# The opening of a two-layer decoder trunk: root on columns of tokens, no POOL, a fourth gate tile, three rounds per tile, unread products on TensorE

## The chip, the cores and the metric

One core of a Trainium2 chip. The metric is the device time of one execution of the whole kernel in microseconds, the median of repeated runs.

## The reference

A trunk of two layers on 512 tokens of 1024 channels, all in float32. Layer 0 mixes tokens by retention (4 heads, rotary positions on q and k), layer 1 by an mLSTM; each is followed by a convolutional FFN. Ahead of each mixer and FFN stands a norm that is modulated by the condition `c`. What matters here is the first of them and the projections that follow it:

```
c_act = silu(c)
mod = c_act @ ada_w[0] + ada_b[0]           # 6 x 1024: shift, scale, gate, twice
h = x * rsqrt(mean(x*x, channels) + 1e-6) * norm_g * (1 + scale) + shift
proj = h @ w_in                             # q, k, v, g
q, k = rope(q, positions), rope(k, positions) / 16
y = group_norm(retention(q, k, v));  x = x + gate * ((silu(g) * y) @ w_out)
```

## The kernel before, in words

**Layout.** Tokens lie along the free axis: `x` is eight tiles of 128 channels by 512 tokens, and a sum over channels is a product with a matrix of ones. Every large product is made of three products of 32-bit operands that are split into a high and a low part (`mm3`, L281 to L283: high x high, low x high, high x low). The high part of a weight is a rounding copy on ACT (L164, in the opening L1165), the low part a subtraction on DVE (L169, in the opening L1169). Activations are split in `parts`: `h.hi` on ACT (L341), `h.lo` on DVE (L343), from `xr`, the scaled tile (L332).

**Modulation.** Each 128 values of `mod` need one pass of DVE over a 128x1025 tile of `ada` (`gemv`, L140: multiply by `silu(c)`, spread on all partitions in `c_ext`, and sum). In the opening three of these are made on POOL (multiply, L144) and ACT (sum, L145) instead. `gain` (L158) is `norm_g * (1 + scale)`, one column.

**The opening** (`ret_start`). Eight tiles of `x` are squared (ACT; the last two on DVE, L1140), pairs are added on DVE (L1145), and four products with ones (L1146) spread the mean of squares to all partitions, 128x512. ACT takes the root (L1190), DVE the reciprocal in two halves (L1196, L1199). Then for each of the eight channel tiles k: two `gemv`s (scale and shift of the tile), `gain`, `scaled`, `parts`, the split of the weight tile `w_s0[k]` (128x896: 512 columns of head 0's values and 3 x 128 of its gate), and 21 products of 512 columns that add into seven PSUM banks: 4 token tiles of values (L1175 to L1177) and 3 gate tiles (L281 to L283). POOL makes the first steps of the tables for the rotary positions meanwhile (`rope_tables`, L1020 to L1034; from L1039 on DVE). DVE, ACT and POOL keep the written order here; PE does not.

**After the opening** the work is a list of items. The first is the projection of the fourth gate tile (`w_in0[7]`), then q and k of head 0 and the first half of head 1's (`proj_item`, 24 products of 512 columns each), and then head 0's scores. A planner orders each engine's instructions by priority (the order of writing) and by its own estimate of when their operands are ready; on an engine they then run in that order. Weights are loaded up to four items ahead into one of six buffers, which the opening's `ada` and weight tiles share. The scores of head 0 need the rotated q and k, and these need the finished tables.

Of the kernel before, what the change touches and what calls it, by code (L numbers as in the profile page):

```python
# [70 lines left out]
def trunk(ctx: ExitStack, tc: tile.TileContext, xT, cb, pos, vec, decay, zmask, ada, w_s0, w_in0, w_v0,  # L71
# [70 lines left out]

    def gemv_pool(layer, f, raw):
        G.tensor_tensor(raw, raw, c_ext[:], op=ALU.mult)  # L144
        A.activation(raw, raw, AF.Copy, accum_out=mods[layer][:, f : f + 1])  # L145
# [871 lines left out]
    def rope_tables():  # L1017

        a, k, k1, r = (slot(n) for n in ("ra", "rk", "rk1", "rr"))
        G.tensor_copy(a[:], posi[:])  # L1020
        G.tensor_scalar(r[:], a[:], col("inv", 0), None, op0=ALU.mult)
        yield
        G.tensor_scalar(k[:], r[:], INV_2PI, None, op0=ALU.mult)
        yield
        ks = []
        for bits in (20, 10):
            big = ROUND * 2.0**bits
            G.tensor_scalar(k1[:], k[:], big, big, op0=ALU.add, op1=ALU.subtract)
            G.tensor_tensor(k[:], k[:], k1[:], op=ALU.subtract)
            yield  # L1030
            ks.append(k1)
            k1 = slot("rk2")
        n = slot("rn")
        G.tensor_scalar(n[:], k[:], ROUND, ROUND, op0=ALU.add, op1=ALU.subtract)  # L1034
        ks.append(n)
        yield
# [10 lines left out]
        turns()  # L1047
        for i, j in ((3, 0), (3, 1), (0, 2), (2, 1), (1, 2), (0, 3), (2, 2), (3, 2)):
            less(i, j)
# [76 lines left out]
    def ret_start():  # L1126

        pss, ps, rs = [], bank("pms"), slot("rs")
        A.activation(rs[:, :1], eps_t[:], AF.Silu)
        one = ones["1"][:1, :].bitcast(F32)  # L1130
        pcs = [bank("pc") for _ in range(2)]
        for i in range(2):
            PE.matmul(pcs[i][:], one, c_row[:1, i * T : i * T + T], start=True, stop=True)
        def mean_squares():
            sq = [slot("sq") for _ in range(KT)]
            for m in range(KT):
                if m < 6:
                    A.activation(sq[m][:], x[m][:], AF.Square)
                else:
                    V.tensor_tensor(sq[m][:], x[m][:], x[m][:], op=ALU.mult)  # L1140
                if m == 5:
                    for i in range(2):
                        A.activation(c_ext[:, i * T : i * T + T], pcs[i][:], AF.Silu)
                if m % 2:
# [37 lines left out]
        with tc.manual_schedule(engines={mybir.EngineType.DVE, mybir.EngineType.Activation, mybir.EngineType.Pool}):  # L1182
# [18 lines left out]
            for k in range(KT):  # L1201
                if k + 1 < KT:
                    for f in (KT + k + 1, k + 1):
                        load_ada(f)
                    if k + 2 < KT:
                        load_raw(k + 2)
# [310 lines left out]
```

## Time and profile before

| | |
|---|---|
| median of 3 runs | 1560.03 us (1559.39 to 1560.14) |
| the profiled execution | 1554.46 us |
| its span, first to last instruction | 1552.7 us |
| mean granted clock of TensorE | 0.992 |
| PE, DVE, ACT, POOL busy | 97%, 77%, 55%, 15% of the span |
| first product of the opening | 16.66 us after the span's start |
| granted clock, 15 to 20 and 20 to 25 us | 0.68 and 0.63 |

PE is TensorE's matmuls, PEld its weight loads, DVE is VectorE, ACT ScalarE, POOL GpSimd, SP the engine whose queue issues the loads. A row of a timeline gives start, length, engine, line, operation, tiles and shapes, and in brackets how long the engine had been idle and what released it. A row of the windows gives a stretch, its length, the busy time and count of instructions of PE, PEld, DVE, ACT and POOL, the granted clock, the DMA share and GB/s. Lengths of matmuls include the time in the pipeline; their pace is read from start to start.

### The profile page before, as it was taken

The page shows a single profiled execution, that of the slowest core. Times are in us where ns is not written, and L with a number is a line of the kernel's source. Part 1 is how long each engine was busy: PE and PEld are TensorE (multiplying, and loading weights), DVE is VectorE, ACT ScalarE, POOL GpSimd, SP SyncE. Part 2 cuts the span into 40 slices and gives each one's busy share as a digit, 9 for nine tenths or more (in the row PEclk, how much of TensorE's full clock was granted, in tenths as well). Part 3 has the DMA queues.
Part 4 walks back from the last instruction along what each step waited for, and adds up shares of the span by engine and source line. Part 5 has one row for each costly group of instructions (what it writes and reads, how often), then busy time and mean ns, then how long its engine had stood idle before and what let it go on. Part 6 is the DMA issues. An engine that isn't in the chain of part 4 may idle for free. (4 is left out here: it accounts for less than half of the span.)

```text
span 1552.7 us, 23173 instructions
## 1 busy us (share of the span) xinstructions
PE 1513.2 (97%) x8996; PEld 1337.2 (86%) x8996; DVE 1200.5 (77%) x1814; ACT 861.2 (55%) x1282; POOL 229.3 (15%) x242
## 2 busy tenths in 40 slices
PE   7999999999999999999999999999999999999997
PEld 4788888888988999998988878888889889999997
DVE  8985768786997878887777777777588977787775
ACT  4534524443456767676655554554545666767763
POOL 3421001110130111111110011001022201111102
PEclk9999999999999999999999999999999999999999
DMA  8753464655315888887444433443312258777751
GB/s 312 228 186 109 143 188 159 204 177 167 110 42 136 210 208 205 230 195 202 160 128 149 149 109 105 152 144 112 126 54 72 67 135 198 195 191 188 187 140 55
DMA packets 72224, 241.79 MB, mean 156 GB/s; under 512 B 9761, under 2 KB 12065, under 8 KB 72114
## 3 DMA queue, kind: packets, MB, share of 16 engines
q1 hardware_dynamic: 59730, 195.22, 38.4%
q0 software_dynamic: 12384, 45.09, 15.3%
q8 instruction: 70, 1.15, 0.3%
q14 instruction: 40, 0.33, 0.1%
HBM read 193.06 MB, written 2.12 MB: 126 GB/s over the span
## 5 line engine op out<-in xcount | busy, mean ns | idle before, releaser
L164 ACT CAST whi<-raw 128x1024 fp32r<-128x1024 f32 (+1 forms) x190 | 194.3, 1029 | 144.4 <-PE pp L282 58.3
L169 DVE TENSOR_TENSOR wlo<-raw,whi 128x1024 fp32r<-128x1024 f32 (+1 forms) x158 | 191.5, 1219 | 46.7 <-ACT whi L164 46.1
L281 PE MATMUL pp<-hh,whi 128*128 128x512 f32 x560 | 218.4, 390 | 2.3 <-DVE vl L278 2.0
L282 PE MATMUL pp<-hl,whi 128*128 128x512 f32 x560 | 218.1, 390 | 0.0
L283 PE MATMUL pp<-hh,wlo 128*128 128x512 f32 x560 | 218.0, 389 | 0.0
L595 DVE SCALAR_TENSOR_TENSOR x<-po,mod,x 128x512 f32<-128x512 f32 (+1 forms) x184 | 114.2, 629 | 71.6 <-PE po L283 68.0
L282 PE MATMUL po<-ggl,whi 128*128 128x512 f32 (+1 forms) x448 | 154.0, 345 | 0.0
L283 PE MATMUL po<-ggh,wlo 128*128 128x512 f32 (+1 forms) x448 | 153.5, 344 | 0.0
L281 PE MATMUL po<-ggh,whi 128*128 128x512 f32 (+1 forms) x448 | 153.0, 345 | 0.0
L422 PE MATMUL p<-hh,whi 128*128 128x256 f32 x544 | 150.6, 277 | 0.0
L423 PE MATMUL p<-hl,whi 128*128 128x256 f32 x544 | 150.4, 276 | 0.0
L424 PE MATMUL p<-hh,wlo 128*128 128x256 f32 x544 | 150.4, 276 | 0.0
L140 DVE SCALAR_TENSOR_TENSOR ada<-ada,c_ext 128x1025 f32<-128x1025 f32 x93 | 115.7, 1245 | 32.3 <-DMA ada<-ada 32.2
L281 PEld LDWEIGHTS pp<-hh,whi 128*128 128x128 f32 x560 | 105.2, 188 | 24.6 <-DVE vl L278 2.5
L283 PEld LDWEIGHTS pp<-hh,wlo 128*128 128x128 f32 x560 | 105.2, 188 | 21.8
L282 PEld LDWEIGHTS pp<-hl,whi 128*128 128x128 f32 x560 | 105.2, 188 | 21.4
L281 PE MATMUL po<-yh,whi 128*128 128x256 f32 (+1 forms) x352 | 115.8, 329 | 0.0
L282 PE MATMUL po<-yl,whi 128*128 128x256 f32 (+1 forms) x352 | 115.6, 328 | 0.0
L283 PE MATMUL po<-yh,wlo 128*128 128x256 f32 (+1 forms) x352 | 115.6, 328 | 0.0
L927 ACT ACTIVATE cv<-p,vecs 128x512 f32<-128x512 f32 x68 | 53.1, 780 | 96.2 <-PE p L424 57.3
L932 DVE SCALAR_TENSOR_TENSOR cv<-p,vecs,cv 128x511 f32<-128x511 f32 (+1 forms) x136 | 101.0, 745 | 2.2
L422 PEld LDWEIGHTS p<-hh,whi 128*128 128x128 f32 x544 | 102.2, 188 | 0.1
(287 smaller groups left out, 3986.9 us busy)
## 6 DMA issues: line engine op xcount, KB each, us to landing
ada<-ada SPq DMA_DIRECT2D x96, 512.5 KB, 4.0
raw<-w_in SPq DMA_DIRECT2D x62, 512.0 KB, 3.8
wb<-w_up SPq DMA_DIRECT2D x34, 512.0 KB, 4.4
wa<-w_up SPq DMA_DIRECT2D x34, 512.0 KB, 5.3
wlo<-wa POOLq DMA_DIRECT2D x34, 512.0 KB, 4.6
wlo<-ws POOLq DMA_DIRECT2D x34, 512.0 KB, 4.9
raw<-w_o SPq DMA_DIRECT2D x32, 512.0 KB, 3.5
raw<-w_dn SPq DMA_DIRECT2D x32, 512.0 KB, 4.4
```

The costliest lines, as they stand in the source:

```text
L140: return V.scalar_tensor_tensor(raw, raw, 1.0, c_ext[:], op0=ALU.mult, op1=ALU.mult, accum_out=mods[layer][:, f : f + 1])
L164: A.copy(hi, w[:, r])
L169: V.tensor_tensor(lo, w[:, r], hi.bitcast(F32), op=ALU.subtract)
L281: PE.matmul(o, ah, bh, start=start, stop=False)
L282: PE.matmul(o, ah, bl, start=False, stop=False)
L283: PE.matmul(o, al, bh, start=False, stop=stop)
L422: PE.matmul(o, hi[:, ch], b[0], start=st, stop=False, skip_group_check=True)
L423: PE.matmul(o, hi[:, ch], b[1], start=False, stop=False, skip_group_check=True)
L424: PE.matmul(o, lo[:, cl], b[0], start=False, stop=sp, skip_group_check=True)
L595: V.scalar_tensor_tensor(x[m][:, r], ps[:, r], gate_col, x[m][:, r], op0=ALU.mult, op1=ALU.add)
L927: A.activation(acc[:], ps[:], AF.Identity, bias=col("fcb", self.layer * 2 * FT + f), scale=self.conv_col(f, 2))
L932: V.scalar_tensor_tensor(acc[:, s:], ps[:, : T - s], self.conv_col(f, j), acc[:, s:], op0=ALU.mult, op1=ALU.add)
```

## The change

- The mean of squares is made the other way round: the squared tile is the loaded weight and one column of ones the moving operand, so that four products per pair give the mean as a 128x4 block, a column for each 128 tokens (`means`). Tiles 0 to 5 are added in pairs, 6 and 7 stand alone. Root and reciprocal are taken on 128x4, four copies of an identity are scaled by the columns, and two products with ones spread the result to 128x512 in PSUM, from which ACT copies it to SBUF.
- POOL has no arithmetic left in the opening: all sixteen `gemv`s are on DVE; the rope tables are wholly on DVE (but for the cosine's last step), and are made after the opening, as item 0 and after the first q product.
- The weight tile holds the fourth gate tile too (128x1024, eight banks); the item `w_in0[7]` goes.
- The 24 products of a tile run in three rounds: high x high for all eight banks, then high x low, then low x high.
- PE keeps the written order in the opening, and 13 products that nobody reads (`busy`) stand between the steps: 5 of 128 columns at the start, 3 after the sums, 5 before the first tile.
- The loads are reordered: an identity and the first columns of `vecs` ahead, the rest of `vecs` after the loads of tiles 0 to 2 but the third weight tile, `posi` last.

```diff
-    def gemv_pool(layer, f, raw):
-        G.tensor_tensor(raw, raw, c_ext[:], op=ALU.mult)
-        A.activation(raw, raw, AF.Copy, accum_out=mods[layer][:, f : f + 1])
...
     def rope_tables():
-        G.tensor_copy(a[:], posi[:])
-        G.tensor_scalar(r[:], a[:], col("inv", 0), None, op0=ALU.mult)
-        yield
-        G.tensor_scalar(k[:], r[:], INV_2PI, None, op0=ALU.mult)
-        yield
+        V.tensor_copy(a[:], posi[:])
+        V.tensor_scalar(r[:], a[:], col("inv", 0), None, op0=ALU.mult)
+        V.tensor_scalar(k[:], r[:], INV_2PI, None, op0=ALU.mult)
         ks = []
         for bits in (20, 10):
             big = ROUND * 2.0**bits
-            G.tensor_scalar(k1[:], k[:], big, big, op0=ALU.add, op1=ALU.subtract)
-            G.tensor_tensor(k[:], k[:], k1[:], op=ALU.subtract)
-            yield
+            V.tensor_scalar(k1[:], k[:], big, None, op0=ALU.add)
+            V.tensor_scalar(k1[:], k1[:], big, None, op0=ALU.subtract)
+            V.tensor_tensor(k[:], k[:], k1[:], op=ALU.subtract)
...
-        G.tensor_scalar(n[:], k[:], ROUND, ROUND, op0=ALU.add, op1=ALU.subtract)
+        V.tensor_scalar(n[:], k[:], ROUND, None, op0=ALU.add)
+        V.tensor_scalar(n[:], n[:], ROUND, None, op0=ALU.subtract)
...
         for i, j in ((0, 0), (1, 0), (0, 1), (2, 0), (1, 1)):
             less(i, j)
         turns()
+        yield
...
     def ret_start():
+        warm = slot("warm", F32R)
+        G.memset(warm[:].bitcast(F32), 1.0)
+        pss, ps = [bank("pst") for _ in range(5)], bank("pms")
+        pcs = [bank("pc") for _ in range(2)]
+        pss += pcs
...
+        def busy(n, w=T):
+            for _ in range(n):
+                PE.matmul(pss[0][:, :w], ones["1"][:], warm[:, :w], start=True, stop=True, skip_group_check=True)
...
+        def means(m):
+            for t in range(4):
+                PE.matmul(ps[:, t : t + 1], sq[m][:, t * P : t * P + P], ones["d"][:, :1].bitcast(F32),
+                          start=(m, t) == (1, 0), stop=m == 7, skip_group_check=True)
+
+        def products(k):
+            hi, lo, st, sp = wh[k], wl[k], k == 0, k == KT - 1
+            h = h0[k]
+            for a, b, first, last in ((h.hi, hi, st, False), (h.hi, lo, False, False), (h.lo, hi, False, sp)):
+                for t in range(4):
+                    PE.matmul(pss[t][:], a[:, t * P : t * P + P], b[:, :T], start=first, stop=last)
+                for j in range(4):
+                    PE.matmul(pss[4 + j][:], b[:, T + j * P : T + j * P + P], a[:], start=first, stop=last)
+
+        with tc.manual_schedule(engines={mybir.EngineType.PE, mybir.EngineType.DVE, mybir.EngineType.Activation,
+                                         mybir.EngineType.Pool}):
+            A.activation(rc[:, :1], eps_t[:], AF.Silu)
+            busy(5, P)
+            for i in range(2):
+                PE.matmul(pcs[i][:], one, c_row[:1, i * T : i * T + T], start=True, stop=True)
+            eye = slot("eye")
+            nc.sync.dma_start(eye[:, :P], ident)
+            nc.sync.dma_start(vecs[:, : VEC["nffn"]], vec[:, : VEC["nffn"]])
+            load_ada(KT)
+            load_ada(0)
+            load_raw(0)
+            load_ada(KT + 1)
+            load_ada(1)
+            load_raw(1)
+            load_ada(KT + 2, aside("ada"))
+            load_ada(2, aside("ada"))
+            nc.sync.dma_start(vecs[:, VEC["nffn"] :], vec[:, VEC["nffn"] :])
+            for m in range(6):
+                square(m)
                 if m % 2:
                     V.tensor_tensor(sq[m][:], sq[m - 1][:], sq[m][:], op=ALU.add)
-                    PE.matmul(ps[:], ones["d"][:].bitcast(F32), sq[m][:], start=m == 1, stop=m == KT - 1)
+                    means(m)
+            square(6)
+            square(7)
+            for i in range(2):
+                A.activation(c_ext[:, i * T : i * T + T], pcs[i][:], AF.Silu)
+            A.activation(rc[:, :1], eps_t[:], AF.Sqrt)
+            means(6)
+            means(7)
+            gemv(0, KT, mod[KT])
+            A.activation(rc[:, :4], ps[:, :4], AF.Sqrt, bias=eps_t[:])
+            V.reciprocal(rc[:, :4], rc[:, :4])
+            diag = slot("diag")
+            busy(3)
             for t in range(4):
                 cs = slice(t * P, t * P + P)
+                V.tensor_scalar(diag[:, cs], eye[:, :P], rc[:, t : t + 1], None,
+                                op0=ALU.mult)
+            for t in range(2):
+                cs = slice(t * HALVES[0][1], (t + 1) * HALVES[0][1])
+                PE.matmul(ps[:, cs], ones["1"][:].bitcast(F32), diag[:, cs], start=True, stop=True,
+                          skip_group_check=True)
+            gain(0, 0, 0)
             gemv(0, 0, mod[0])
             high(0)
+            busy(5)
+            xr = slot("xr")
+            for p in HALVES:
+                r = slice(*p)
+                scaled(0, r, ps, 0, 0, xr=xr)
+                A.activation(h0[0].hi[:, r], xr[:, r], AF.Identity, bias=mods[0][:, :1])
+            low(0)
+            V.scalar_tensor_tensor(h0[0].lo[:], xr[:], mods[0][:, :1], h0[0].hi[:].bitcast(F32),
+                                   op0=ALU.add, op1=ALU.subtract)
+            A.copy(rs[:], ps[:])
+            pss.append(bank("pst"))
             for k in range(KT):
                 if k + 1 < KT:
-                    for f in (KT + k + 1, k + 1):
-                        load_ada(f)
                     if k + 2 < KT:
                         load_raw(k + 2)
+                    if k + 3 < KT:
+                        load_ada(KT + k + 3)
+                        load_ada(k + 3)
                     high(k + 1)
                     gemv(0, KT + k + 1, mod[KT + k + 1])
                     gain(0, 0, k + 1)
-                    xr = scaled(k + 1, slice(None), rs, 0, 0)
-                    (gemv_pool if k + 1 in (2, 4, 6) else gemv)(0, k + 1, mod[k + 1])
-                    parts(h0, k + 1, slice(None), xr, 0, 0, lambda: low(k + 1))
-                if 0 < k < 6:
-                    next(tables, None)
+                    gemv(0, k + 1, mod[k + 1])
+                    parts(h0, k + 1, slice(None), scaled(k + 1, slice(None), rs, 0, 0), 0, 0, lambda: low(k + 1))
                 products(k)
+            nc.sync.dma_start(posi[:], pos.broadcast_to([P, T]))
...
-    ret_start()
-    proj_item(w_in0[7], h0, ret_gate(0))
+    tables = rope_tables()
+    item([], lambda w: next(tables))
+    ret_start()
...
     def ret_q(i, between=nothing):
+        if not i:
+            between = lambda j: item([], lambda w: next(tables, None)) if not j else None
```

81 lines of the change are left out of this document (22 added, 59 removed).

## The prediction, as put on record before the result

> **What bounds the kernel now.** I read the page first, then the windows, then each engine's timeline of the first 110 us.
>
> ```profile
> PE 1513.2 (97%) x8996; PEld 1337.2 (86%) x8996; DVE 1200.5 (77%) x1814; ACT 861.2 (55%) x1282; POOL 229.3 (15%) x242
> ```
>
> PE is the bound nearly everywhere, so a change to the opening is worth only what PE loses there. The windows of the opening, of the 32.6 us after it, and of DVE's stretch that I need below (sum of each engine's busy time, then PEclk, the DMA share and GB/s):
>
> ```profile
> 16.66:24.66 8.00, 7.38 (x18) 5.24 (x19) 7.32 (x12) 1.93 (x3) 1.79 (x1) 0.57 1.02 406
> 24.66:75.43 50.77, 44.49 (x176) 34.58 (x175) 49.38 (x61) 24.46 (x36) 26.21 (x14) 0.93 0.74 239
> 65.09:107.78 42.69, 42.69 (x190) 35.37 (x189) 36.86 (x51) 23.26 (x36) 9.07 (x9) 1.00 0.59 196
> 75.43:108.06 32.63, 32.63 (x145) 27.03 (x144) 27.94 (x39) 14.66 (x23) 6.43 (x6) 1.00 0.55 178
> ```
>
> PE's timeline (start, length, and in brackets the idle time before it and its releaser):
>
> ```profile
> 16.66 0.66 PE L1175 MATMUL pst<-whi,hh 128*128 128x512 f32 x1 [4.17 <-ACT hh L341]
> ...
> 23.76 0.39 PE L283 MATMUL pst<-hh,wlo 128*128 128x512 f32 x1
> ...
> 39.61 0.51 PE L1177 MATMUL pst<-whi,hl 128*128 128x512 f32 x1 [2.04 <-DVE hl L343]
> ...
> 75.20 0.39 PE L283 MATMUL pp<-hh,wlo 128*128 128x512 f32 x1
> ...
> 108.06 0.39 PE L281 MATMUL psc<-qkh,qkh 128*128 128x512 f32 x1
> ```
>
> The first product starts at 16.66. The opening's 168 products and the 24 of the fourth gate tile (the item that follows) end at 75.20 + 0.23 = 75.43. From there to the first scores at 108.06 six items of 24 take 32.63 us: 5.44 us an item, 0.227 a product. So 192 products need 43.5 us and take 58.8: **15.2 us are lost**. The clock explains about 7 (8.00 us at 0.57 lose 3.4; 50.77 at 0.93 lose 3.6), waits for DVE and ACT the rest (PE is busy 44.49 of the 50.77; the one before 39.61 is the longest of these). DVE and POOL show why:
>
> ```profile
> 9.30 1.29 DVE L1140 TENSOR_TENSOR sq<-x 128x512 f32<-128x512 f32 x2
> ...
> 13.80 1.74 DVE L1196 RECIPROCAL rs<-rs 128x256 f32<-128x256 f32 x1
> ...
> 23.95 3.29 DVE L1169 TENSOR_TENSOR wlo<-raw,whi 128x896 fp32r<-128x896 f32 x1
> ...
> 57.48 1.08 DVE L1169 TENSOR_TENSOR wlo<-raw,whi 128x896 fp32r<-128x896 f32 x1
> ...
> 59.15 1.21 DVE L140 SCALAR_TENSOR_TENSOR ada<-ada,c_ext 128x1025 f32<-128x1025 f32 x1
> ...
> 61.02 0.68 DVE L1039 SCALAR_TENSOR_TENSOR rr<-rk,rr 128x512 f32<-128x512 f32 x1
> 61.62 0.74 DVE L332 SCALAR_TENSOR_TENSOR xr<-x,gain,rs 128x512 f32<-128x512 f32 x1
> ...
> 65.09 0.42 DVE L1042 TENSOR_SCALAR rk<-rr 128x512 f32<-128x512 f32 x1
> 65.43 1.22 DVE L169 TENSOR_TENSOR wlo<-raw,whi 128x1024 fp32r<-128x1024 f32 x1
> ...
> 107.10 0.68 DVE L278 TENSOR_TENSOR qkl<-rp,qkh 128x512 fp32r<-128x512 f32 x1
> ```
>
> ```profile
> 22.86 3.43 POOL L144 TENSOR_TENSOR ada<-ada,c_ext 128x1025 f32<-128x1025 f32 x1 [22.42 <-DMA ada<-ada]
> ```
>
> The same low-part subtraction takes 3.29 us beside POOL's product (23.95 falls in 22.86 to 26.29) and 1.08 us with POOL idle. The reciprocal at 13.80 and its like for the other half, 3.5 us, stand on DVE's way through the first tile.
>
> **The change, part by part.**
>
> *1. Head (before the first product).* The root of 128x4 replaces the root and reciprocals of 128x512. But the sum over channels becomes four products of one column each for five tiles (1, 3, 5, 6, 7), with a square tile as the loaded weight. Rows that come near: the old sums with their loads, the spacing of the narrowest products, the `c` products, and ACT's last steps before the first product:
>
> ```profile
> L1146 PEld LDWEIGHTS pms<-sq,ones_d x8: 186/288/334, 6.2 to 11.5; 128*128 128x128 f32 x8
> L1146 PE MATMUL pms<-sq,ones_d x8: 593/867/1222, 6.2 to 11.9; 128*128 128x512 f32 x8
> ```
>
> ```profile
> 111.44 0.28 PE L283 MATMUL psc<-qkh,qkl 128*128 128x256 f32 x1
> 111.56 0.28 PE L281 MATMUL psc<-qkh,qkh 128*128 128x256 f32 x1
> ```
>
> ```profile
> 2.48 3.75 PE L1133 MATMUL pc<-c_row,ones 1*128 1x512 f32 x4 [2.48 <-DMA c_row<-cb]
> ```
>
> ```profile
> 14.25 0.94 ACT L1165 CAST whi<-raw 128x896 fp32r<-128x896 f32 x1 [0.97 <-DMA raw<-w_s]
> 16.10 0.51 ACT L341 ACTIVATE hh<-xr,mod 128x256 fp32r<-128x256 f32 x1 [0.91 <-DVE xr L332]
> ```
>
> Four old products show eight loads, so a tile of four makes 8 passes. The trace has no one-column product. A pass costs at least the 0.12 us between 256-wide products (111.44 to 111.56), and at most the longest load, 0.334, if nothing overlaps: 1.0 to 2.7 us a tile. I take 0.16, between the spacing and the shortest load (0.186), nearer the first since loads overlap products throughout: 1.3 us a tile. PE is free of the `c` products at 6.2; tile 5 is summed when the squares at 9.30 start, and the last square, earlier by one, is done at about 10. Then tile 5 ends at 10.7, tile 6 at 12.0, tile 7 at 13.3 (bounds 12.4, and 6.2 + 5 x 2.7 = 19.7). From there: root 0.3 and reciprocal 0.2 (estimates, below ACT's 0.51 for 256 columns and far below the 1.74 for 256), four scaled identities of 128 columns 0.7 and the gain 0.2 (estimates, below the 0.42 that a single-input DVE step of 512 columns takes), one gemv 1.25, scaling of half a tile 0.5 (0.74 for a whole one), its high part 0.51: 3.7 us. Beside it PE spreads the diagonal (two products of half the old width, two passes each at 0.3 to 0.6: 1.2 to 2.4 us) and does five unread products (1.1 at full pace, 2.1 at half). First product at **17.0**, bounds 16.0 and 24.8 (19.7 + 5.1 with PE cold). The identity (0.07 MB) ahead of the loads is made up for by `vecs` (0.25 MB), most of which now follows the first weight tile; that tile's cast began at 14.25, before its columns are needed. Since PE now keeps the written order, a sum that waits for its square holds up only the opening's own products; and ACT's copy of the spread root (some 0.7) is hidden beside the first tile's products, else it would cost itself.
>
> *2. Clock.* After the 4.17 us gap the cold pace lasted from 16.66 to 23.76, 7.1 us, and cost 3.4. Now thirteen unread products and the diagonal keep PE at work from about 13 on, so part of that time passes before any product that counts: I take **1.5 us** lost, bounds 0 and 3.4. The Trainium skill ("TensorE: Matmul & The Clock Gate", Part 1) says that the full clock is granted only after a sustained busy window of about 3.4 us, and that the window is free-running, so a start may need up to two. By that rule the lead-in of some 4 us makes the loss between 0 and about 1.5 us, which would move the sum by at most 1.5; the trace's 7.1 us agrees with two windows rather than one.
>
> *3. Pace of the tiles.* PE's 24 products a tile: 5.44 us. DVE's last tile in the old opening, without POOL: 59.15 to 65.09 is 5.94, less two rope steps (0.6 each by 61.02 to 61.62) is 4.74, plus 0.14 for 1024 columns (1.22 against 1.08) is 4.88. That tile had both its gemvs on DVE, as every tile has now. So DVE leads PE by 0.56 a tile and PE is the bound, waits gone.
>
> ```profile
> ada<-ada SPq DMA_DIRECT2D x96, 512.5 KB, 4.0
> ```
>
> Loads ask 2 x 512.5 + 512 KB a tile, 1.57 MB in 5.44 us, 289 GB/s; the window at 16.66 moved 406, so they hide. SP's queue now waits for a buffer of an earlier tile before each load; behind it stand only later tiles' loads and `posi`, which are needed a tile or more later. Were the rate 239 as in the second window, a tile would take 6.6 us and seven of them 8 us more.
>
> *4. Fourth gate tile, rounds, PE's order.* The product count stays; 24 move from an item into the tiles. The round order lets high parts run first, which hides the first low part (1.2 us) under 8 products (1.8 us). All eight PSUM banks now end together; the first ends 1.6 us before the opening does and ACT empties it meanwhile: 0, at most 0.4.
>
> So the opening ends at 17.0 + 43.5 + 1.5 = **62.0** instead of 75.43: **-13.4**.
>
> *5. Rope tables on DVE, afterwards.* They are 32 DVE instructions: 18 with two inputs at 0.6 and 14 single ones at 0.34 (65.09 to 65.43), 15.6 us; after the old opening DVE had 11 and 5 left, 8.3. DVE thus gets 7.3 us more between its last tile and the first scores, and 1.2 less (the gate tile's low part). In the old run PE starts the scores at 108.06, and the last split they need ends at 107.10 + 0.68 = 107.78: **0.28 us of slack**. New: DVE's first low part ends at about 18.6, its last tile 7 x 4.88 later, 52.8; the scores are due at 62.0 + 32.6 = 94.6, 41.8 later. DVE's old 42.69 become 48.8, of which 5.8 were idle (42.69 - 36.86) and can be filled: 43.0 to 48.8. PE is short by 1.2 to 7.0 us, unless the next head's projections go first (nothing but the planner's order forbids it): then 0. I take **+1.5**, bounds 0 and 8.
>
> Sum: 1554.46 - 13.4 + 1.5 = 1542.6 for the profiled execution. The median of the runs shown, 1560.03, is 5.57 above; the same stage is saved in both, so **1548.1**.
>
> **Rivals.**
> *A. DVE decides the scores:* nothing is filled or reordered, the full 7.0 to 8 us are waited: 1560.0 - 13.4 + 7.5 = 1554.1. For it: the 0.28 us; against: DVE's idle 5.8 us.
> *B. One-column products are slow:* 0.334 a pass, cold: first product at 24.8, the opening ends at 24.8 + 43.5 + 1.5 = 69.8, a gain of 5.6 less the 1.5: 1555.9. For it: the `c` products took 0.94 us each (3.75 for 4), cold, just before this place. Against: loads overlapped everywhere else.
> *C. The unread products do not raise the clock* (the change doesn't do what it says): the old 3.4 are lost again, 1550.0. For it: the trace has no unread product. Against: at 23.76 the clock rose under the very same width of product.
> *D. Slower: the loads decide.* Place: SP's queue, where each load now waits for one of six buffers. Up to the last weight tile 2.1 (x) + 0.3 + 8 x 1.57 = 15.0 MB must land from about 2.2 us on, and the last tile needs some 8.5 us after that (cast 1.0, low part 1.1, products 5.44, hand-overs). The opening then ends over 3.1 us later than 75.43 once the mean rate falls under 15.0 / (78.5 - 8.5 - 2.2) = 221 GB/s; at 210 it ends at 82.1 and the time is 1566.7. For it: the second window's 239 GB/s. Against: there the DMA share was 0.74, the engines had nothing more to fetch, and at 16.66 they moved 406.
>
> **How the numbers follow.** Forecast 0.62, A 0.14, B 0.12, C 0.07, D 0.05. Lower end: first product 16.0, no cold loss, no wait: opening ends at 59.5, 1560.0 - 15.9 = 1544.1. Upper end: A and B reach 1554 to 1556; I take 1556.3, which leaves out D and what of A and B would come together. A measurement here tells about 0.2% (3.1 us) from no change. Faster takes the forecast, C, A and most of B: 0.90; within 0.2% the rest of B and half of D: 0.06; slower 0.04.
>
> **What would show it.** Head: first counted product near 17, five groups of one-column products of about 1.3 us each. Clock: 1.00 in PEclk within 3 us of that product. Pace: tiles 5.44 us apart on PE, DVE's low parts all near 1.2 us. End of the 192 products near 62. Tables: DVE busy without gaps to about 90, and PE's idle before the first scores 0 to 3 us. Wrong would be: PE waiting for `ada` loads, for low parts after 62, or a second cold stretch.

## The result, and the profile after

The changed kernel takes **1563.22 us** (median of 20 runs, 1559.48 to 1567.36) against 1560.09 for the kernel before (20 runs, 1556.58 to 1563.12): ratio 1.0021, 95% interval 1.0013 to 1.0030. The change costs 3.1 us where 12 us of gain were forecast.

The opening gained nearly what was forecast, and what was moved behind it took the gain away again. First the page's row of the engines in the changed kernel, which differs from that of before by 28 us less on POOL, 6 less on DVE, 6 more on PE and 10 more on PEld:

```profile
PE 1519.6 (97%) x9045; PEld 1346.8 (86%) x9045; DVE 1194.1 (76%) x1830; ACT 859.2 (55%) x1277; POOL 201.4 (13%) x232
```

PE's timeline of the head (start, length, tiles; where a row has no bracket, PE did not wait; a counted product is one that is read):

```profile
6.40 8.88 PE L1164 MATMUL pms<-ones_d,sq 128*128 128x1 f32 x40
15.14 1.63 PE L1136 MATMUL pst<-warm,ones 128*128 128x512 f32 x3
16.57 2.00 PE L1217 MATMUL pms<-diag,ones 128*128 128x256 f32 x4
18.01 2.69 PE L1136 MATMUL pst<-warm,ones 128*128 128x512 f32 x5
20.50 1.19 PE L1172 MATMUL pst<-whi,hh 128*128 128x512 f32 x4
```

Forty passes of one column take 8.88 us, 0.222 each. The first counted product comes at 20.50, later than in the kernel before (16.66), but the first four take 1.02 us from start to start (20.50 to 21.52), and 0.91 at full pace: they run close to the full pace.

The windows of the opening, of the stretch from its last product to the first scores, and of DVE from the end of its last tile to the second half of the rotated k (same columns as before: stretch, busy time of PE, PEld, DVE, ACT, POOL, granted clock, DMA share, GB/s):

```profile
20.50:64.16 43.66, 43.66 (x194) 36.16 (x193) 42.02 (x64) 18.83 (x23) 0.17 (x1) 1.00 0.86 297
64.16:109.99 45.83, 32.84 (x146) 26.84 (x144) 37.84 (x58) 19.10 (x29) 6.91 (x9) 0.88 0.48 167
57.32:109.97 52.65, 39.67 (x175) 32.47 (x173) 43.27 (x63) 22.97 (x34) 7.06 (x9) 0.90 0.55 190
```

In the first row PE is busy for the whole 43.66 us at clock 1.00: 192 products without a wait. The opening ends at 64.16 instead of 75.43, **11.3 us earlier**. In the second row PE works 32.84 of 45.83 us. Where the 13 us are lost, PE's timeline shows:

```profile
109.99 0.80 PE L277 MATMUL psc<-qkh,qkh 128*128 128x512 f32 x1 [12.99 <-ACT qkh L273]
110.58 0.63 PE L278 MATMUL psc<-qkl,qkh 128*128 128x512 f32 x1
...
116.94 0.40 PE L277 MATMUL pp<-hh,whi 128*128 128x512 f32 x1
```

The first scores wait **12.99 us** for the rotated q and k. They then start cold, that is at a lower pace (0.59 us from the first product to the second, 0.23 at full pace), and take 6.95 us (109.99 to 116.94) instead of the 3.86 of before (108.06 to 111.92): **3.1 us more**. The sum -11.3 + 13.0 + 3.1 is +4.8, and the scores do end 5.0 us later than in the profile of before. What the wait waited for, on DVE, POOL and ACT:

```profile
57.32 4.63 DVE L165 TENSOR_TENSOR wlo<-raw,whi 128x1024 fp32r<-128x1024 f32 x4
...
68.75 0.75 DVE L558 SCALAR_TENSOR_TENSOR vl<-vt,vm,vh 128x512 fp32r<-128x512 f32 x1 [0.86 <-ACT vh L557]
...
73.03 0.75 DVE L558 SCALAR_TENSOR_TENSOR vl<-vt,vm,vh 128x512 fp32r<-128x512 f32 x1
73.69 0.42 DVE L1016 CAST ra<-posi 128x512 f32<-128x512 int32 x1
...
98.49 0.43 DVE L1049 TENSOR_SCALAR rr<-rr 128x512 f32<-128x512 f32 x1
98.84 1.22 DVE L165 TENSOR_TENSOR wlo<-raw,whi 128x1024 fp32r<-128x1024 f32 x1
101.50 0.69 DVE L1057 TENSOR_TENSOR rp<-pp,cos 128x512 f32<-128x512 f32 x1 [1.44 <-POOL cos L1053]
```

```profile
109.32 0.62 ACT L273 CAST qkh<-rp 128x512 fp32r<-128x512 f32 x1 [3.30 <-POOL rp L1061]
```

The tables begin at 73.69, behind the last of the four value splits (vl), which came one after the other from ACT and POOL, and end at 98.49; sine, cosine and rotation take another 11 us to the last high part at 109.32.

A second loss stands far behind the change, in layer 1. PE's, SP's and DVE's timelines:

```profile
887.75 0.80 PE L277 MATMUL pav<-sh,vh 128*128 128x512 f32 x1 [4.46 <-ACT sh L273]
```

```profile
880.00 0.33 SPq L178 DMA_DIRECT2D raw<-w_in  x1
880.42 0.38 SPq L1339 DMA_DIRECT2D mb<-scratch  x1
```

```profile
884.96 0.35 DVE L1346 SCALAR_TENSOR_TENSOR w<-mb,bcols,zm 128x128 f32<-128x128 f32 x1 [3.11 <-DMA mb<-scratch]
```

The small load `mb` that weighs layer 1's scores is issued at 880.42, right behind a weight load. The scores stand at 868.37, so it comes 12 us after them, where the kernel before issued it 2.7 us after (867.70, scores at 864.97). PE waits 4.46 us and then goes on cold (0.43 us from 889.07 to the next start). From layer 1's first scores to the end the changed kernel needs 695.8 us (1564.2 - 868.37), the kernel before 687.7 (1552.7 - 864.97): 8.1 more in this pair of traces.

The pair differs by 11.5 us and the medians by 3.1, because the profiled execution of before (1554.46) lies below nearly all of its plain runs and that of the changed kernel (1566.02) above its median. A second profile of before has a span of 1558.5; from the start of the last head's weighted values in layer 0 (pav, near 362) to the second FFN's norm (near 770) it needed 408.0 us, the first 404.1. Of these 3.9 us, 3.1 lie in the first 48 products: 11.84 us instead of 8.76, cold after waits of 1.4 us in all. In the other kernels of this study the same 48 take 8.4 to 13.0 us and the whole stretch 402 to 409, so no difference of two traces in that stretch is read as an effect below.

### The profile page after: what moved, and what is told of

Same layout as the page of the kernel before. It is cut to its first block, busy times and chain, and to the rows that moved or that the text cites. A ratio compares the mean times of both kernels' runs of the same rounds, so it can differ in the third digit from the quotient of the medians.

```text
span 1564.2 us, 23264 instructions
## 1 busy us (share of the span) xinstructions
PE 1519.6 (97%) x9045; PEld 1346.8 (86%) x9045; DVE 1194.1 (76%) x1830; ACT 859.2 (55%) x1277; POOL 201.4 (13%) x232
## 4 chain that ended last, share of the span: by engine, by line
PE 70%; DVE 18%; ACT 4%; issue 4%; DMA 2%; POOL 1%; SPq 0%; DVEq 0%; ACTq 0%; POOLq 0%
PE po L277 7%; PE po L278 7%; PE po L279 7%; PE p L418 7%; PE p L420 7%; PE p L419 7%; PE pp L277 5%; PE pp L278 5%; PE pp L279 5%; DVE wlo L165 3%; PE pv L578 2%; PE pv L580 2%; PE pv L579 2%; DVE ada L140 2%; DVE hl L339 1%
## 5 line engine op out<-in xcount | busy, mean ns | idle before, releaser
L277 PE MATMUL pp<-hh,whi 128*128 128x512 f32 x552 | 215.2, 390 | 0.4 <-DVE vl L274 0.4
L278 PE MATMUL pp<-hl,whi 128*128 128x512 f32 x552 | 214.9, 389 | 0.0
L279 PE MATMUL pp<-hh,wlo 128*128 128x512 f32 x552 | 214.8, 389 | 0.0
```

The lines of the kernel that those rows point to most:

```text
L277: PE.matmul(o, ah, bh, start=start, stop=False)
L278: PE.matmul(o, ah, bl, start=False, stop=False)
L279: PE.matmul(o, al, bh, start=False, stop=stop)
```

## The experiments

Each is an edit of the changed kernel unless it says otherwise. Ratios are to the kernel before, timed beside it.

**Is it the tables?** Their range reduction is left out: of the 32 steps on DVE, 29 go, and copy, multiply and clamp stay.

```diff
         V.tensor_copy(a[:], posi[:])
         V.tensor_scalar(r[:], a[:], col("inv", 0), None, op0=ALU.mult)
-        V.tensor_scalar(k[:], r[:], INV_2PI, None, op0=ALU.mult)
...
         V.tensor_scalar(r[:], r[:], pi, -pi, op0=ALU.min, op1=ALU.max)
```

> The changed kernel with the rope tables cut to three DVE steps (the range reduction of the angles is left out). Theory T, the place of the tables: the 13.0 us that PE waits ahead of the first scores, and the 3.1 us of half clock behind it, come from the 15.6 us of table steps on DVE; without them PE does not wait there: 1563.2 - 16.1, about 1547. Rival D, the opening is no gain in itself or the wait has another cause (loads, banks): the time stays at 1560 or above. Rival L, the later order in layer 1 costs as much: about 1552 to 1555.

Measured 1547.52 us, ratio 0.9923 (0.9907 to 0.9939). That is the 1547 expected. The wait before the scores is gone, a wait of 4.41 in layer 1 is still there. So the rewritten opening gains, and the 29 steps take it back.

**Is it that the positions are loaded last?** Their load goes from behind the opening to behind tile 2's `ada`.

```diff
+            nc.sync.dma_start(posi[:], pos.broadcast_to([P, T]))
...
-            nc.sync.dma_start(posi[:], pos.broadcast_to([P, T]))
```

> The changed kernel with one load moved: the positions are loaded in the opening's head instead of at its end. Theory T (the tables stand on DVE behind the four value splits, because of the order in which they are written, not because their operand is late): the table steps still begin near 74 us and the time stays within 3 us of 1563. Rival P, the positions land too late: the tables begin near 58 us and the time falls to about 1550.

Measured 1563.08 us, 1.0020 (1.0008 to 1.0031). The tables begin at 75.12, again behind the value splits, and the wait is 14.47. The load was not what they waited for; their place in DVE's order is.

**Put them in front, ACT's steps too.** Positions early, all steps in the written order of the opening, behind its last tile (the tables' two items go).

```diff
             products(k)
+            for _ in rope_tables():
+                pass
...
-    tables = rope_tables()
-    item([], lambda w: next(tables))
```

> The changed kernel with the positions loaded in the head and all 32 table steps on DVE in the opening's written order, directly after the last tile's low part and ahead of the value splits; nothing is left out. Theory T, the place: the steps run from about 58 to 82 us with low parts between them, the rotated k is ready near 97, PE waits at most 3 us ahead of the scores: about 1550. Rival W, the amount of DVE work: the scores wait as long as now, 1560 or above.

Measured 1576.92 us, 1.0109 (1.0093 to 1.0125), a miss. ACT's and PE's timelines show why:

```profile
85.95 0.63 ACT L1050 ACTIVATE sin<-rr 128x512 f32<-128x512 f32 x1 [19.04 <-DVE rr L1049]
```

```profile
88.39 0.79 PE L277 MATMUL pp<-hh,whi 128*128 128x512 f32 x1 [23.86 <-ACT vt L554]
```

ACT keeps the written order as well. It stood 19 us at the sine while the value and gate banks waited to be emptied behind it, and PE had no free bank.

**The same, but only DVE's steps in front.** The 32 steps in the written order behind the last tile, sine and cosine as item 0, the positions early as in the last two.

```diff
             products(k)
+            next(tables)
...
-    item([], lambda w: next(tables))
+    item([], lambda w: next(tables, None))
```

> The changed kernel with the positions loaded early and the 32 DVE steps of the tables in the written order right behind the last tile's low part, ACT's three steps as item 0 (so that ACT empties the value banks first, which the run before this one did not let it do); as many items as in the kernel before. Theory T, the place: low parts interleave, the steps end near 83 us, PE waits 0 to 5 us ahead of the scores, the later stall goes too: 1550 to 1555. Rival W, the amount of DVE work: the scores wait 10 us or more, 1560 or above.

Measured 1555.50 us, 0.9974 (0.9962 to 0.9987). PE's timeline has two waits left:

```profile
66.28 0.50 PE L277 MATMUL pp<-hh,whi 128*128 128x512 f32 x1 [1.72 <-ACT vt L554]
...
103.19 0.79 PE L277 MATMUL psc<-qkh,qkh 128*128 128x512 f32 x1 [3.72 <-ACT qkh L273]
```

The wait before the scores fell from 13 to 3.7, with the same arithmetic on the same engine. The early positions alone did not shorten it (14.47), and nor does the number of items, which is that of before here (with an empty item alone the wait is 15.16, below): the order of writing set it.

**Spread them over the opening.** Nine steps in the head, one or two per tile, sixteen behind; the positions and the whole of `vecs` are loaded behind the first `ada` tile.

```diff
             gemv(0, KT, mod[KT])
+            next(tables)
...
+                if 0 < k < 7:
+                    next(tables)
                 products(k)
+            next(tables)
```

> As the run beside it, but with nine of the table steps in the head (where DVE waited 3.4 us for the root), two or one in each of tiles 2 to 7, and 16 behind the last tile; positions and all of vecs are loaded behind the first ada tile. Theory T: the head costs nothing, tiles take up to 5.6 us on DVE (1 us over all), the tables end near 77 us and PE does not wait ahead of the scores: 1547 to 1550. Rival: the loads put ahead delay the first weight tile by 1.3 us and the opening with it, 1552 or above.

Measured 1554.90 us, 0.9972 (0.9959 to 0.9985): no better than the last. PE's first counted products, and DVE in the head:

```profile
22.37 1.91 PE L1175 MATMUL pst<-whi,hh 128*128 128x512 f32 x4
```

```profile
13.92 0.43 DVE L1018 TENSOR_SCALAR rk<-rr 128x512 f32<-128x512 f32 x1
14.38 0.43 DVE L1022 TENSOR_SCALAR rk<-rk 128x512 f32<-128x512 f32 x1
```

The head is 1.9 us longer. The nine steps were meant for a gap of 3.35 us in which DVE waited for the root, and they take 4.88 (12.68 to 17.56). Steps that each need the one before start 0.46 us apart where the forecast had 0.34 (65.09 to 65.43 in the profile of before), and 0.29 is a wait for `vecs`. The wait at the scores is 3.03.

**The other way round: the kernel before, its tables moved to DVE behind the opening.**

```diff
-            G.tensor_scalar(k1[:], k[:], big, big, op0=ALU.add, op1=ALU.subtract)
+            V.tensor_scalar(k1[:], k[:], big, None, op0=ALU.add)
+            V.tensor_scalar(k1[:], k1[:], big, None, op0=ALU.subtract)
...
+    tables = rope_tables()
+    item([], lambda w: next(tables))
```

> The kernel before with this one part of the change: the rope tables wholly on DVE as items after the opening. Theory T: the opening gains a little from POOL's absence in the tables (1 to 3 us), the tables then start behind the value splits at about 77 us and end 20 us later, and PE, which had 0.28 us of slack, waits 6 to 12 us ahead of the scores and loses 3 us of clock: 1565 to 1573. Rival: the tables' place costs nothing of its own: 1557 to 1561.

Measured 1561.40 us, 1.0007 (0.9996 to 1.0017), a miss in size: the old opening is some 5 us shorter without the tables in it (PE is done at 102.95, 110.74 - 7.79, with what the scores of before followed at 108.06), then the scores wait 7.79 us. The two nearly cancel: the scores come at 110.74, and at 108.06 and 109.48 in the two profiles of before.

**The tables back on POOL in the new opening**, the positions early and an empty item in place of the tables' two (see next).

```diff
-            V.tensor_scalar(k1[:], k[:], big, None, op0=ALU.add)
-            V.tensor_scalar(k1[:], k1[:], big, None, op0=ALU.subtract)
+            G.tensor_scalar(k1[:], k[:], big, big, op0=ALU.add, op1=ALU.subtract)
...
+                if 0 < k < 6:
+                    next(tables, None)
```

> The new opening with the tables left where the kernel before had them (on POOL and VectorE within the opening), with one empty item so that the later items keep their places. If the move of the tables is what took the gain, TensorE does not wait at the scores, VectorE's low parts beside POOL's steps are longer again and the opening 3 to 6 us longer than in the changed kernel: 1543 to 1545 + 3 to 6 = 1546 to 1551. Rival: the scores come late for another reason than the tables (the value splits, the low parts), and the time is 1557 to 1561.

Measured 1556.55 us, 0.9983 (0.9971 to 0.9996), between the two expectations. DVE's low part of the activations beside POOL and without it, and PE's wait at the scores:

```profile
32.10 1.79 DVE L339 SCALAR_TENSOR_TENSOR hl<-xr,mod,hh 128x512 fp32r<-128x512 f32 x1
...
40.00 0.74 DVE L339 SCALAR_TENSOR_TENSOR hl<-xr,mod,hh 128x512 fp32r<-128x512 f32 x1
```

The step takes 1.09 and 1.79 us in the two tiles during POOL's steps (22.96 to 40.3) and 0.74 after them. Waits of 1.73 and 1.63 in the tiles and 2.62 before the scores remain. The tables are dear in either place: without their 29 steps the kernel takes 1542.10 (below).

**Layer 1.** One empty item. The change takes one item out of the list (the fourth gate tile) and puts two in (the two parts of the tables), so every later item stands one place further on. With the empty item it is two places, and the later items are back on their odd or even places.

```diff
     item([], lambda w: next(tables))
+    item([], lambda w: None)
```

> The changed kernel with one empty item more in the planner's list, so that the later items fall on the same odd and even places as before (every second item carries one side gemv of layer 1). Theory R, a ripple: the 4.5 us that PE waits in layer 1 for the scores' weights, whose loads stand behind a weight load on SP's queue, come from the shifted places: 1558 to 1559. Rival: that wait has to do with the opening's own timing, and the time stays within 2 us of 1563.

Measured 1560.44 us, 1.0014 (1.0003 to 1.0024). In layer 1 `mb` is issued 2.7 us after the scores and PE does not wait:

```profile
874.37 0.38 SPq L1340 DMA_DIRECT2D mb<-scratch  x1
```

The wait of 4.46 is gone, and from layer 1's scores to the end it takes 687.7 us, as before. At the head, though, the scores come at 112.73 instead of 109.99, with a wait of 15.16; the median falls by 2.8 us. The traces of all kernels here agree on the odd and even places. Where the later items stand one place further on (the changed kernel, the one with early positions, the cut tables without the empty item) or one place back (all steps in the written order, ACT's too), `mb` is issued 12.05 us after the scores, and from these to the end it takes 693.1 to 697.2 us. Where they stand on their old place or two further on, it is 2.7 us after, and 687.3 to 689.6 us. The same item in the kernel with the cut tables:

> The kernel with the cut tables and one empty item more, so that the later items keep their odd or even places (range reduction left out). It still waits 4.4 us in layer 1 in its trace. If that wait is a cost of its own, it goes (to below 1 us) and the time falls from 1547.5 to 1543 to 1545.5 (the empty item took 2.8 off the changed kernel). If the shift is given back later in the kernel whatever the places are, the time stays at 1547 to 1548.

Measured 1542.10 us, 0.9888 (0.9875 to 0.9900): 5.4 us less than with the cut tables alone, more than expected. So **the shift by one place costs 5.4 us** here (from layer 1's scores to the end 693.5 and 688.1 us in the two traces), and it is a cause of its own beside the wait at the first scores. Why the planner sets the load behind a weight load in the one case and ahead of it in the other was not tried. PE between the opening and the scores in this kernel, for comparison with the second window of the changed one:

```profile
64.16:97.19 33.03, 33.03 (x148) 27.35 (x146) 23.54 (x32) 18.67 (x30) 8.19 (x9) 1.00 0.62 225
```

No idle time at all. Against the kernel with the same empty item and all tables, 1560.44, the tables' 29 steps thus cost **18.3 us**; the pair without the empty item gives 15.7 (1563.22 and 1547.52).

**The unread products.** Taken out of the kernel with the cut tables, where PE decides the head's worth.

```diff
-            for _ in range(n):
+            for _ in range(0):
```

> The kernel with the cut tables, in which TensorE never waits before the scores, now also without the thirteen unread products (range reduction of the rope angles left out, as in the kernel with the cut tables). If the unread products raise the clock, the first counted products run cold as they did in the kernel before, where the cold stretch of 7.1 us cost 3.4: the granted clock is under 1 for 3.4 to 7 us after about 20.5, and the time is 1547.5 + 1.5 to 3.4 = 1549.0 to 1550.9. If the forty one-column passes and the spreading of the diagonal warm the clock by themselves (rival C: the unread products do nothing), it is 1547.0 to 1548.0.

Measured 1547.67 us, 0.9920 (0.9908 to 0.9932), against 1547.52 with them: no difference that these runs can tell from nothing. PE's first counted products, in their timeline:

```profile
19.94 2.08 PE L1142 MATMUL pst<-whi,hh 128*128 128x512 f32 x4 [1.12 <-ACT hh L1197]
```

They run cold at first (2.08 for four against 1.19; the first seven take 3.08 us from start to start), but start 0.56 earlier, since the five unread products in front (18.01 to 20.50, themselves at the cold pace) made them wait. The 192 products take 45.03 us instead of 43.66, and the opening ends at 64.97, 0.8 later than in the changed kernel; this is too little to show in the medians. The column of the granted clock reads 1.00 in both cases here; the pace of the products shows the difference.

**ACT instead of VectorE.** Positions behind the second part of `vecs`, the first part of `vecs` behind the first `ada` tile; eight single-input steps on ACT, none of the tables in the head, an even spread over the tiles, and the mean of the value split scaled on ACT.

```diff
-        V.tensor_scalar(r[:], a[:], col("inv", 0), None, op0=ALU.mult)
-        V.tensor_scalar(k[:], r[:], INV_2PI, None, op0=ALU.mult)
+        A.activation(r[:], a[:], AF.Copy, scale=col("inv", 0))
+        A.activation(k[:], r[:], AF.Copy, scale=INV_2PI)
...
-            V.tensor_scalar(k1[:], k[:], big, None, op0=ALU.add)
+            A.activation(k1[:], k[:], AF.Identity, bias=bigs[:, 2 * b : 2 * b + 1])
...
-        G.tensor_scalar(m[:], m[:], -1.0 / DV, None, op0=ALU.mult)
+        A.activation(m[:], m[:], AF.Copy, scale=-1.0 / DV)
```

> The tables spread over the opening, with eight of their single-input steps on ACT instead of VectorE (ACT is idle some 3 us a tile there), none of them in the head, and the mean of the value split scaled on ACT instead of POOL. If VectorE's queue alone sets the scores, the head comes back to 20.5 (from 22.4), VectorE ends the tables by about 86 (from 89.5), the wait before the scores is 1 to 3 us and the time 1550 to 1553 (the spread kernel: 1554.9). Rival: ACT's added steps hold back its high parts, TensorE waits for them in tiles 2 to 4, and the time is 1554 to 1557.

Measured 1554.12 us, 0.9960 (0.9948 to 0.9973): the rival's range. The head is back (first product at 19.97), but the tiles wait 1.76, 0.37 and 1.39 us for ACT's high parts and the scores 2.41.

**Is the wait itself the loss?** The versions with short waits lie only 4 to 6 us below the kernel with the empty item, of the 18.3. Two gate projections of the second head are put ahead of the first scores, the tables left where the change put them (with the empty item):

```diff
                 proj_item(w_in0[i * 8 + 2 * n + j], h0, then)
+                if (i, n, j) == (1, 0, 1):
+                    ret_g(1, range(2))
                 between(2 * n + j)
```

> The changed kernel with one empty item (1560.4) and with two of the second head's gate projections put ahead of the first scores, all steps of the tables where they were. If TensorE's wait at the scores is the loss, it falls from 15.2 by 10.9 (two items of 24 products), less 1.2 to 2.4 for the two low parts that VectorE now has to do first: 5 to 7 us are left, the time is 1560.4 - 8.5 to 10 = 1550 to 1552. Rival: what VectorE has to do for the tables costs the same wherever TensorE's work stands (its later low parts and splits come late instead), and the time is 1558 to 1561. This settles also whether 'the next projections first' in the forecast needed only another order.

Measured 1552.00 us, 0.9949 (0.9934 to 0.9963), 8.4 us less than the same kernel without it. PE at the first scores:

```profile
110.47 0.50 PE L277 MATMUL psc<-qkh,qkh 128*128 128x512 f32 x1 [2.17 <-ACT qkh L273]
110.80 0.39 PE L278 MATMUL psc<-qkl,qkh 128*128 128x512 f32 x1
```

The scores come no later than before the edit (110.47 against 112.73) with 10.9 us more work done, the wait is 2.17 and the pace near full at once. So the wait and the cold products behind it are a loss, but not all of it: 1552.00 is still 9.9 us above the kernel with the cut tables and the same item (1542.10). Of the 9.7 us between these two traces, 2.4 lie at the first scores (110.47 less 10.9, against 97.19) and 5.0 between these and the last head's weighted values (357.05 and 349.68). In that stretch PE waits 3.4 us in short waits where the other kernel has none. So the rival holds in part: the tables' steps still cost time behind the scores. To which steps these short waits go back was not traced. The control, the kernel before with the same two items in front:

> Control: the kernel before with the same two projections ahead of the first scores. There TensorE does not wait at the scores, so the order should be worth nothing: ratio 0.999 to 1.001. If the order is worth something of its own (loads, the later scores), it shows here, and that much has to be taken off the other two.

Measured 1561.41 us, 1.0007 (0.9997 to 1.0017): no effect, as expected, since PE did not wait there. And the version with ACT's steps:

> The same two projections ahead of the first scores, in the kernel with the tables spread over the opening and eight of their steps on ACT (1554.1; there the wait at the scores is 2.4 us, with a colder clock after it). If the wait and the clock after it are the loss, the wait goes and the time is 1550 to 1552. Rival: 1553.5 to 1555, the order makes no difference there.

Measured **1548.19 us**, 0.9926 (0.9912 to 0.9940), 5.9 less than without and below the expected range. Its scores start at 112.62 without a wait:

```profile
112.62 0.39 PE L277 MATMUL psc<-qkh,qkh 128*128 128x512 f32 x1
112.85 0.39 PE L278 MATMUL psc<-qkl,qkh 128*128 128x512 f32 x1
```

It is the fastest version here with the full computation, 12.6 us below the kernel before beside it (1560.82). A second profile of the kernel before served for the comparison above:

> The kernel before once more, for a second trace: its first profiled execution, 1554.46, lies under all of its plain runs (1555.92 to 1562.97). Either the spread of some 5 us sits in a few long waits that this trace shows and the other doesn't, or it is spread evenly.

Measured 1560.26 us, span 1558.5. Of the 5.8 us between the two profiles 1.4 are there at the first scores and 3.1 come in the last head's weighted values.

## Why the prediction was wrong, point by point

**Step 5 failed: the price of the tables on DVE.** It stood at +1.5 with bounds 0 and 8; the trace has 13.0 of wait and 3.1 of cold products. DVE's busy time was counted within 2 us: the forecast had 43.0, or 48.8 with the idle time, from the end of its last tile to the last low part; the window 57.32 to 109.97 has 43.27 busy, and 44.96 up to 111.80, where the last low part ends. Three things were wrong around it.
- *The idle time.* The forecast let 5.8 idle microseconds be filled, since DVE had work waiting. The window has 52.65 - 43.27 = 9.4 of idle. These are hand-overs, and nearly the same as in the old window: DVE waited for ACT's high parts of the weights (2.2 us before, 3.7 now), of the rotated q and k (1.7 and 1.7) and of the value splits (1.4 and 1.7), and for the cosine (0.5 and 1.4). The largest of them, DVE's group of weight low parts with its idle time last, in the kernel before (65.09 to 107.78), the changed one (57.32 to 109.97) and the one with only DVE's steps in front (57 to 103):

```profile
L169 DVE TENSOR_TENSOR wlo<-raw,whi 128x1024 fp32r<-128x1024 f32 x13 | 15.8, 1217 | 2.2 <-ACT whi L164 2.2
...
L165 DVE TENSOR_TENSOR wlo<-raw,whi 128x1024 fp32r<-128x1024 f32 x13 | 15.6, 1223 | 3.7 <-ACT whi L160 3.7
...
L165 DVE TENSOR_TENSOR wlo<-raw,whi 128x1024 fp32r<-128x1024 f32 x11 | 13.4, 1219 | 0.0
```

  In the changed kernel the planner's order put the tables behind the value splits, which come from a chain over three engines; the tables' steps could have filled the waits ahead of 73.69, but came behind them. POOL's part of that chain is one number per partition; its timeline in the changed kernel:

```profile
67.06 0.90 POOL L555 TENSOR_SCALAR vm<-vm 128x1 f32<-128x1 f32 x1 [2.40 <-ACT vt L554]
69.38 0.21 POOL L555 TENSOR_SCALAR vm<-vm 128x1 f32<-128x1 f32 x1 [1.41 <-ACT vt L554]
```

  DVE waited 0.86 and 0.87 us ahead of two of the four value splits, 0.84 and 0.83 at the rotated high parts, and 1.44 for the cosine. Dependent steps 0.46 apart added some tenths. The reordered kernel shows that the filling itself was possible: with the table steps in front, DVE's waits for weight high parts and value splits are 0.0, and PE's wait is 3.7 instead of 13 us.
- *The start.* DVE reached the item weights at 57.32, not 52.8: 4.5 late. The head gives 2.6 of it (the first tile's low parts are done at 21.2, not 18.6), a tile pace of 5.00 instead of 4.88 gives 0.8, and an item's weight that went ahead of the last tile's low part (at 55.52) 1.1. PE was ready for the scores 2.4 late itself (97.00, not 94.6). With 52.65 us of DVE's work and waits against 48.8 at most: 7.0 (the forecast's longest wait) + 4.5 + 3.9 - 2.4 = 13.0, which is what the trace shows.
- *The clock.* The forecast priced a wait at its length. After 13 us of idle time the scores took 3.1 us more, and the kernel with the two gate items in front shows both going together.

"Unless the next head's projections go first" was the escape that the forecast gave itself at no price. Nothing forbade it, but nothing did it either: it takes an edit of the order of items, and with it the wait falls to 2.17 us and the time by 8.4, to 1552.00 and not to the kernel without the tables. Rival A had the right mechanism with too short a wait (7.5).

**The head (step 1) was 3.5 us too early.** A one-column pass took 0.222 us, not 0.16: 40 of them 2.5 us more, of which the sums ended 2.0 later than forecast (15.3 against 13.3). The rest lies between the sums and the first product, 5.2 us where 3.7 were forecast. 0.56 of it is the queue of unread products, by the kernel without them.

**The clock (step 2) was better than forecast**, about 0.1 us lost instead of 1.5, but the unread products are worth little. Without them 1.4 us of pace are lost and 0.56 are gained by the earlier start, and the medians do not differ. Rival C did not occur: its 3.4 us of cold loss stayed away with the unread products, and without them too. Which of the other products ahead, the one-column passes or the diagonal, keeps the cold time shorter than the old 7.1 us is not shown. The Trainium skill ("TensorE: Matmul & The Clock Gate", Part 1) has the full clock granted after a sustained busy window of about 3.4 us. With the products, PE was busy without a gap from 6.40 on and the unread ones at 18.01 to 20.50 were still at 0.50 us each; the trace does not fit the rule if the one-column passes count as busy, and can fit it only if the count begins with the wide products at 15.14, some 5 us before the full pace; no run here separates the two.

**Pace, loads and banks (steps 3 and 4) were right.** 192 products in 43.66 us against 43.5, no wait for `ada` (297 GB/s in the window), low parts all near 1.22 us. The banks cost nothing in this trace; in two others the first product behind the opening waited for one to be emptied (1.20 us with the cut tables, 0.76 with the empty item), more than the 0.4 of step 4. B and D did not occur.

**Not foreseen at all: layer 1.** The step "24 products move from an item into the tiles" was priced by its products alone, and the tables by their steps. One item out of the list and two in shifted every later item by one place, and a small load went behind a weight load 800 us later: 5.4 us by the pair with the cut tables, 2.8 by the pair with all tables.

**The sum by experiments.** Opening, clock and pace without tables and without the shift: 1542.10, which is 18.0 below before. The traces place 10.9 to 12.3 of that at the scores (97.19 against 108.06 and 109.48); the rest lies where runs of one kernel differ by 4 us, and is not settled. Tables on DVE +18.3; the shift of items +2.8: 1563.2. These are differences of medians along one chain of kernels and close by construction; along the other chain they are 5.4 for the shift and 15.7 for the tables. Of the tables' price, 8.4 go with the wait at the first scores; the rest is only in part traced.

## What to carry to other kernels

Work that is moved off a busy stretch has to be laid out again on its new engine instruction by instruction, with what stands ahead of it in that engine's order and the hand-overs it waits for; busy time alone said 43 us, and the end came 9 us of idle time later. Where TensorE must wait, look for work that can go ahead of the wait before making the waiting chain shorter: two projections moved by three lines gained 8.4 us over the kernel with the empty item, more than any of the four ways to place the tables (3.9 to 6.3). And an item put into a planned list or taken out of it can move loads far behind it, so check the waits of the whole trace, not of the stage that was edited.

## What the runs showed of the hardware that was not expected

- A pass of one column in float32 with a 128x128 tile as the weight took 0.222 us (8.88 for 40). The products of 512 columns right behind it, at the cold pace, took 0.48 (15.14 to 16.57), so one column cost about half of 512; it is nearly what a 512-column product takes at the full pace (0.227). What such a pass takes at the full pace no run shows.
- A DVE step of 512 columns that reads the result of the one before starts 0.46 us after it, one with independent work behind it 0.34; two-input steps show 0.72 and 0.60 (85.19 to 85.91 and 79.44 to 80.04 in the changed kernel).
- The granted clock read 1.00 in the windows 15 to 20 of the changed kernel and 20 to 22 of the one without unread products, while products went at about half pace (0.50 and 0.47 from start to start); the spacing of starts told more than the column.
- In the new opening with tables on POOL, DVE's 0.74 us step took up to 1.79 beside POOL's steps, as the low part did in the kernel before (3.29 against 1.08).
